# Two places for the weights of 256-column matmuls, and the last tile's transposes behind a unit of matmuls

## The chip, the cores and the metric

One NeuronCore of a Trainium2 chip runs the whole program. The metric is the device time of one execution in microseconds; the time given is the median of three runs. Matmuls run on TensorE, their results are in PSUM banks of 512 float32 per partition, and VectorE and ScalarE read them from there. SP issues the loads of the weights, GpSimd a few stores and memsets.

## The reference

A trunk of two layers on 512 tokens of 1024 channels, all float32. Layer 0 mixes tokens by stick-breaking attention (16 heads), layer 1 by a gated MLP over chunks of 128 tokens; behind each stands a SwiGLU feed-forward block of inner width 2816:

```
h = rms_norm(x, pre_g) * (1 + scale) + shift        # scale, shift, gate from c
y = mixer(h)            # attention in layer 0, gated token MLP in layer 1
x = x + gate * rms_norm(y, post_g)
h = rms_norm(x, ffn_pre_g) * (1 + scale') + shift'
y = (silu(h @ w_gate) * (h @ w_up)) @ w_down
x = x + gate' * rms_norm(y, ffn_post_g)
```

## The kernel before

**Precision.** A float32 operand is split into a high part in fp32r (ScalarE, a Copy) and a low part, the rest (VectorE, a subtraction). `mm3` makes three matmuls of each product: high by high, high by low, low by high. In the profile, wh and wl are the parts of a weight tile, hTh and hTl those of the transposed activations, Sh and Sl those of sums of them.

**Weights.** `stream` lists all weight tiles in the order of their use. `wload` issues the load of the next into `raw` (two buffers); `wemit` splits it into the buffers that `wtile` hands out in turn: five, and a sixth (`wpool2`) from the end of the attention on, each 1088 float32 long, one for the high and one for the low part. A tile has 1024 elements; `at` says how many elements into its buffer it begins. Tiles whose matmuls have 256 columns (`wgu`, `win_u` and the block tiles) begin at `SHORT` = 29, most others at 16, those of `down_blocks` at 0. `wget(key, look)` takes a tile and emits the splits of `look` more.

**Feed-forward.** The first three pairs of gate and up slabs are plain units (`Ffn.unit`): 48 matmuls of 256 columns into a bank `gu` for 256 tokens. The other 19 are done by `seven`, which makes seven half-size products where eight would be needed, 84 matmuls of 256 columns into banks r1 to r3, from block tiles `x`, `t13`, `t24` and `b21` that `blocks` works out of two raw loads (rawx, rawy). `b21` has its own buffers of 544 elements, two for each part.

**Boundary.** `out_proj` ends a sublayer. Its last four slabs of weights are used tile by tile of 128 tokens (tt = 0 to 3), and behind each tile stands `boundary`: ScalarE squares y (`junk<-y`), VectorE forms t = y * G, then x (`x<-t,r,x`), ScalarE squares x (`junk<-x`), VectorE forms t from x, A and B (this last operation is kept as `feature[0]`), TensorE transposes t in eight pieces (`tp<-identt,t`), and both halves are split into hTh and hTl. While the last two tiles go through it, TensorE has work on the first 256 tokens of the next sublayer, handed over as `nxt`: three plain units of gu, or two steps of v and one of u ahead of the gated MLP. `nxt[0]` stands ahead of the boundary of tile 2, `nxt[1]` ahead of that of tile 3, `nxt[2]` behind it.

**Order.** The order of each engine's work is set by a list scheduler when the program is built, by priority in program order and an estimate of when an operation is ready. `order(b, a)` holds b behind a without a wait. In the attention and in the `seven` stage the order on TensorE and VectorE is chained as written.

**Attention.** For each of eight head pairs, scores (`z`), scans on VectorE (`left<-ga,ones`), transposes (`tw`), splits (`ar`) and products with the values (`av`) alternate with steps of `filler`, three 512-column matmuls each: first the q and k of later pairs (`pqk`), then the first products of the output projection (`y`). `FILLS` gives the steps of each of seven slots for pairs 0 to 4, `LAST` for pairs 5 to 7. The sixth slot stands between the last flips and the scores of the next pair's last block; the first slot behind the pair's first transposes, the second behind the next pair's first scores.

Of the kernel before, what the change touches and what calls it, by code (L numbers as in the profile page):

```python
# [10 lines left out]
AF = mybir.ActivationFunctionType  # L11
# [15 lines left out]
SEVEN = ((2, 4, 6, 7, 9), (2, 4, 6, 7, 9, 10))  # L27
NLAST = 3

SHORT = 29  # L30


@with_exitstack
def trunk(ctx: ExitStack, tc: tile.TileContext, A: dict, out: bass.AP):
# [17 lines left out]
    def nm(s):  # L52
        uid[0] += 1
        return f"{s}_{uid[0]}"
# [7 lines left out]
    pe = {"prev": None, "chain": False}  # L62

    class Vector:


        chain, prev = False, None
# [13 lines left out]
    class Scalar:  # L81


        chain, prev = False, None
# [8 lines left out]
    act = Scalar()  # L93

    def pe_op(b):

        if pe["chain"] and pe["prev"] is not None:
            order(b, pe["prev"])
        pe["prev"] = b

    def order(b, before):
        tc.add_manual_dep(
            b.ins, before.ins.name,
            mybir.DependencyInfo(mybir.DependencyClass.NoSync, mybir.DependencyReason.DATA),
            reason="order",
        )
# [7 lines left out]
    last_tp = [None]  # L114

    def transpose(o, i):
        last_tp[0] = nc.tensor.transpose(o, i, ident)  # L117
        pe_op(last_tp[0])
# [18 lines left out]
    turn = [-1]  # L137
    wpools = [(wpool, 5)]
    fwork = {}
    last_low = [None]  # L140
# [3 lines left out]
    def wload():  # L144

        src, a, b, key = stream[len(raws)]
        if src is None:
            raws.append(block_loads(key[1]))
            return
        raw = wraw.tile([P, a, b], F32, tag="raw", name=nm("raw"))  # L150
        load(raw[:], src)
        raws.append(raw)

    def wemit():
        n = len(got)
        src, a, b, key = stream[n]
        if len(raws) == n:
            wload()
        if src is None:
            if not first_blocks or n > first_blocks[-1] + KF:  # L160
                first_blocks.append(n)
            for _ in blocks(*next_raws(n)):
                pass
            return
        raw = raws[n]
        if key[0] == "wdn" and key[2] in SEVEN[key[1]]:
            got.append(down_blocks(raw))
            return
        h, l = wtile(a, b, SHORT if key[0] in ("wgu", "win_u") else 16)
        if key[0] == "wqk" and key[1]:  # L170

            act.activation(h[:], raw[:], AF.Copy)
            nc.vector.tensor_tensor(l[:], raw[:], h[:].bitcast(F32), ALU.subtract)
            if len(raws) == n + 1 and stream[n + 1][3][0] == "wqk":
                wload()
        else:
            act.activation(h[:], raw[:], AF.Copy)
            last_low[0] = nc.vector.tensor_tensor(l[:], raw[:], h[:].bitcast(F32), ALU.subtract)  # L178
        got.append((h, l))

    def wtile(a, b, at=0):
        turn[0] = (turn[0] + 1) % sum(c for _, c in wpools)
        pool = wpools[0][0] if turn[0] < wpools[0][1] else wpools[1][0]
        return [
            pool.tile([P, 1088], F32R, tag=n, name=nm(n))[:, at : at + a * b].rearrange(
                "p (a b) -> p a b", a=a
            )
            for n in ("wh", "wl")
        ]
# [20 lines left out]
    def blocks(xr, yr):  # L210

        fp = fwork["pool"]

        def high(t, src):
            act.activation(t[0][:], src, AF.Copy)

        def low(t, src):
            dve.tensor_tensor(t[1][:], src, t[0][:].bitcast(F32), ALU.subtract)

        def half(t, i):  # L220
            return lambda k: (t[0][:, 4 * i + k, :], t[1][:, 4 * i + k, :])

        x = wtile(KD, P, SHORT)
        high(x, xr[:])
        f13 = fp.tile([P, KD, P], F32, tag="f13", name=nm("f13"))
        sum13 = dve.tensor_tensor(
            f13[:].rearrange("p (a k) f -> p a (k f)", a=2),
            xr[:].rearrange("p (a k) f -> p a (k f)", a=2),
            yr[:, 4:8, :].rearrange("p (a k) f -> p a (k f)", a=1).to_broadcast([P, 2, 512]),
            ALU.add,  # L230
        )
        if len(got) == first_blocks[-1]:
            order(sum13, feature[0])
        yield
        b21 = [
            fp.tile([P, 544], F32R, tag=f"b21{i}", name=nm("b21"))[
                :, SHORT : SHORT + 512
            ].rearrange("p (a b) -> p a b", a=4)
            for i in range(2)
        ]  # L240
        high(b21, yr[:, 0:4, :])
        t13 = wtile(KD, P, SHORT)
        high(t13, f13[:])
        f24 = fp.tile([P, KD, P], F32, tag="f24", bufs=1, name=nm("f24"))
        dve.tensor_tensor(f24[:, 0:4, :], f13[:, 0:4, :], xr[:, 4:8, :], ALU.add)
        dve.tensor_tensor(f24[:, 4:8, :], f24[:, 0:4, :], yr[:, 0:4, :], ALU.add)
        yield
        low(x, xr[:])
        low(b21, yr[:, 0:4, :])
        yield  # L250
        t24 = wtile(KD, P, SHORT)
        high(t24, f24[:])
        low(t13, f13[:])
        yield
        low(t24, f24[:])
        got.append({
            "B11": half(x, 0), "B22": half(x, 1), "B21": half(b21, 0),
            "T1": half(t13, 0), "T3": half(t13, 1), "T2": half(t24, 0), "T4": half(t24, 1),
        })

    feature = [None]
    first_blocks = []

    def ahead():
# [219 lines left out]
        lo %= 256  # L484
        return h[:, k % 4, lo : lo + n], l[:, k % 4, lo : lo + n]

    def boundary(s, tt, y, xin, hT, S, tag):

        halves = [slice(0, 512), slice(512, D)]
        sq = [small.tile([P, 1], F32, tag=f"sq{hf}", name=nm("sq")) for hf in range(2)]  # L490
        t = npool.tile([P, D], F32, tag="n", name=nm("t"))
        for hf, c in enumerate(halves):
            act.activation(junk[:, c], y[hf][:], AF.Square, accum_out=sq[hf][:])
            if hf == 1:
                sd, r2 = rms(sq[1][:], sq[0][:])
            dve.tensor_tensor(t[:, c], y[hf][:], ada["G", s][:, c], ALU.mult)
        dve.reciprocal(r2[:], sd[:])
        x = xin(tt)
        dve.scalar_tensor_tensor(x[:], t[:], r2[:, 0:1], x[:], ALU.mult, ALU.add)
        xd[tt] = dram.tile([P, D], F32, tag=f"x{tt}", bufs=2, name=nm("xd"))  # L500
        nc.gpsimd.dma_start(out=xd[tt][:], in_=x)
        sx = small.tile([P, 1], F32, tag="sx", name=nm("sx"))
        act.activation(junk[:], x[:], AF.Square, accum_out=sx[:])
        sd, r1 = rms(sx[:])
        dve.tensor_tensor(t[:], x[:], ada["A", s], ALU.mult)
        dve.reciprocal(r1[:], sd[:])
        feature[0] = dve.scalar_tensor_tensor(
            t[:], t[:], r1[:, 0:1], ada["B", s], ALU.mult, ALU.add
        )
        late = []  # L510
        for q in range(2):
            ps = bank("tp", tag)
            for k in range(4):
                kk = q * 4 + k
                transpose(ps[:, k * P : (k + 1) * P], t[:, kk * P : (kk + 1) * P])
            a = ps[:].rearrange("p (a b) -> p a b", a=4)
            if tt % 2 == 0:
                hT[tt // 2, q] = (slot(F32R, "hTh", 4, 256), slot(F32R, "hTl", 4, 256))
            c = slice(tt % 2 * P, (tt % 2 + 1) * P)
            th, tl = hT[tt // 2, q]  # L520
            split(th[:, :, c], tl[:, :, c], a)
            if S is not None and tt < 2:
                if tt == 0:
                    S["c", q] = slot(F32, "c", 4, 256)
                act.activation(S["c", q][:, :, tt * P : (tt + 1) * P], a, AF.Copy)
            late.append(a)
        return lambda: sums(S, tt, late)
# [33 lines left out]
    def out_proj(s, nk, get_act, wkey, J, bg, hT, nxt=(), pre=None, S=None, steps=0, bg2=None):  # L561
# [6 lines left out]
        mid = min(nk - J, -(-8 * len(bg.parts) // steps) + 1) if steps else None  # L568
        yp = None
        y = [[None, None] for _ in range(NT)]  # L570
# [39 lines left out]
        xin = xs.get  # L610
# [10 lines left out]
                xs[tt + 2] = x_load(tt + 2)  # L621
        evacs, late = [], []
        for n, tt in enumerate((2, 3)):
            if nxt:
                evacs.append(nxt[n]())
            late.append(boundary(s, tt, y[tt], xin, hT, S, "p" if tt == 3 else "b"))
        if nxt:
            evacs.append(nxt[2]())
            with tc.issue_after(last_sqrt[0].ins):
# [51 lines left out]
    hT = new_hT()  # L681
# [153 lines left out]
    with tc.tile_pool(name="att", bufs=1) as att, tc.tile_pool(name="att2", bufs=2) as att2:  # L835
# [44 lines left out]
        NEARLY = 4  # L880
        FIRST = (8, 9)
        FILLS = (2, 3, 2, 2, 2, 2, 3)
        LAST = (2, 2, 2, 2, 2, 1, 1), (1, 2, 1, 1, 1, 1, 1), (2, 0, 2, 0, 2, 2, 0)
        fgen = filler()

        def fill(n, at=None):
# [9 lines left out]
        for js in (B31, B2, B0):  # L896
            at, n = {}, 0
# [134 lines left out]
        for k in range(KD):  # L1032
# [9 lines left out]
            if k > 3:  # L1042
                tt = TURNS[k - 4]
# [17 lines left out]
        for i in range(NPAIR):  # L1061
            scores, flip, values, gather, part = cur
            more = i + 1 < NPAIR
            F = iter(FILLS if i < 5 else LAST[i - 5])
            flip(LATE, 0)
# [50 lines left out]
    junk = jpool.tile([P, D], mybir.dt.bfloat16, name="junk")  # L1116
# [532 lines left out]
```

## Time and profile before

| | |
|---|---|
| runs | 1106.79, 1112.53, 1112.93 us; median 1112.53 |
| profiled execution | 1114.39 us |
| its span | 1112.6 us |
| its granted TensorE clock | 0.997 |
| busy: TensorE, VectorE, ScalarE | 1090.5, 945.9, 593.1 us |
| DMA | 176.38 MB, mean 159 GB/s |

The profile is that of one execution. A group's row gives line, engine, operation, out<-in by the program's names, shapes and count, then the busy time and the mean duration of one in ns, then the idle time of the engine ahead of them and what ended it. A row of the timeline gives start and duration in us, and in brackets the idle time ahead of it with what ended it. A matmul overlaps the next one, so the rate is read from the distance of starts, or from a stretch divided by its count. L109 is the line in `mm` that issues every matmul, L117 the transposes, L87 ScalarE, L71 VectorE, L178 the low part of a streamed weight tile.

### The profile page before, as it was taken

How to read it: one execution, taken by the hardware profiler on the slowest of the kernel's cores; microseconds unless marked ns; L12 is line 12 of the kernel's file. 1: busy time of each engine (PE TensorE's matmuls, PEld its weight loads, DVE VectorE, ACT ScalarE, POOL GpSimd, SP SyncE). 2: the span in 40 equal slices, each digit the busy share in tenths (PEclk: the TensorE clock that was granted, in tenths of full speed). 3: DMA queues.
4: the chain of work that ended last, by engine and by line, in shares of the span. 5: the costliest groups of instructions: out<-in, count | busy, mean ns of one | idle time of the engine just before them, and what ended most of it. 6: DMA issues, size and time to landing. Idle time of an engine off the chain costs nothing.

```text
span 1112.6 us, 18514 instructions
## 1 busy us (share of the span) xinstructions
PE 1090.5 (98%) x7404; PEld 982.9 (88%) x7404; DVE 945.9 (85%) x1248; ACT 593.1 (53%) x982; POOL 29.5 (3%) x53
## 2 busy tenths in 40 slices
PE   6999999999999999999999999999999999999997
PEld 4787878788999999998888889988999999989995
DVE  4988999876989999989866967668979999899996
ACT  5445565665655555554243627426555555565652
POOL 0020100000000000000000000001000000000000
PEclk9999999999999999999999999999999999999999
DMA  8966433214423434459757465234334343332243
GB/s 303 363 224 212 137 124 117 92 57 151 153 98 126 163 127 151 133 186 356 272 190 259 138 228 183 82 116 160 120 110 160 125 162 104 107 112 95 79 140 123
DMA packets 51355, 176.38 MB, mean 159 GB/s; under 512 B 6074, under 2 KB 9146, under 8 KB 51268
## 3 DMA queue, kind: packets, MB, share of 16 engines
q1 hardware_dynamic: 48708, 166.81, 43.9%
q0 software_dynamic: 2560, 8.39, 2.0%
q8 instruction: 58, 0.95, 0.3%
q14 instruction: 29, 0.24, 0.1%
HBM read 164.69 MB, written 8.39 MB: 156 GB/s over the span
## 4 chain that ended last, share of the span: by engine, by line
PE 82%; DVE 9%; ACT 4%; DMA 3%; issue 2%; SPq 0%; DVEq 0%; ACTq 0%
PE r L109 31%; PE y L109 17%; PE v L109 8%; PE pqk L109 7%; PE u L109 4%; PE gu L109 4%; PE av L109 2%; PE z L109 2%; PE tw L117 1%; DMA raw<-in_wdn 1%; DVE wl L71 1%; DVE al L71 1%; PE tp L117 1%; DVE wl L178 1%; PE ab L109 1%
## 5 line engine op out<-in xcount | busy, mean ns | idle before, releaser
L87 ACT ACTIVATE wh<-raw 128x1024 fp32r<-128x1024 f32 (+1 forms) x112 | 115.7, 1037 | 136.8 <-PE y L109 38.7
L109 PE MATMUL r<-Sh,wh 128*128 128x256 f32 x608 | 168.1, 276 | 0.0
L109 PE MATMUL r<-Sh,wl 128*128 128x256 f32 x608 | 167.9, 276 | 0.0
L109 PE MATMUL r<-Sl,wh 128*128 128x256 f32 x608 | 167.9, 276 | 0.0
L109 PE MATMUL y<-wh,as 128*128 128x512 f32 x480 | 150.0, 390 | 0.0
L178 DVE TENSOR_TENSOR wl<-raw,wh 128x1024 fp32r<-128x1024 f32 x87 | 105.9, 1222 | 48.5 <-ACT wh L87 47.8
L109 PEld LDWEIGHTS r<-Sh,wh 128*128 128x128 f32 x608 | 114.1, 188 | 0.3 <-ACT e L87 0.2
L109 PEld LDWEIGHTS r<-Sl,wh 128*128 128x128 f32 x608 | 114.2, 188 | 0.1
L109 PEld LDWEIGHTS r<-Sh,wl 128*128 128x128 f32 x608 | 114.1, 188 | 0.0
L109 PEld LDWEIGHTS y<-wh,as 128*128 128x128 f32 x480 | 90.0, 188 | 18.7
L71 DVE TENSOR_TENSOR wl<-f,wh 128x1024 fp32r<-128x1024 f32 x87 | 103.3, 1221 | 1.4 <-ACT wh L87 1.4
L87 ACT ACTIVATE wh<-f 128x1024 fp32r<-128x1024 f32 x87 | 91.8, 1056 | 20.0 <-DVE f L71 11.8
L87 ACT ACTIVATE e<-r 128x256 f32<-128x256 f32 x114 | 43.8, 385 | 102.6 <-PE r L109 100.4
L109 PE MATMUL y<-wl,as 128*128 128x512 f32 x240 | 93.7, 390 | 0.0
L109 PE MATMUL r<-hTh,wh 128*128 128x256 f32 x304 | 84.2, 277 | 0.2 <-DVE gu L71 0.2
L109 PE MATMUL r<-hTh,wl 128*128 128x256 f32 x304 | 84.0, 276 | 0.0
L109 PE MATMUL r<-hTl,wh 128*128 128x256 f32 x304 | 84.0, 276 | 0.0
L109 PE MATMUL r<-hTh,b 128*128 128x256 f32 x304 | 58.0, 276 | 0.0
L109 PEld LDWEIGHTS r<-hTh,wh 128*128 128x128 f32 x304 | 57.1, 188 | 0.9 <-DVE gu L71 0.9
L87 ACT ACTIVATE wh<-rawx 128x1024 fp32r<-128x1024 f32 x38 | 40.5, 1065 | 32.0 <-PE r L109 29.0
L109 PEld LDWEIGHTS r<-hTl,wh 128*128 128x128 f32 x304 | 57.1, 188 | 0.0
L109 PEld LDWEIGHTS r<-hTh,wl 128*128 128x128 f32 x304 | 57.1, 188 | 0.0
(260 smaller groups left out, 2943.6 us busy)
## 6 DMA issues: line engine op xcount, KB each, us to landing
rawada<-in_ada SPq DMA_DIRECT2D x80, 512.0 KB, 5.8
rawy<-in_wy SPq DMA_DIRECT2D x38, 512.0 KB, 4.4
rawx<-in_wx SPq DMA_DIRECT2D x38, 512.0 KB, 4.2
raw<-in_wdown SPq DMA_DIRECT2D x22, 512.0 KB, 5.5
raw<-in_wdn SPq DMA_DIRECT2D x22, 512.0 KB, 3.7
raw<-in_wqk SPq DMA_DIRECT2D x16, 512.0 KB, 4.1
ada<-in_ada0p SPq DMA_DIRECT2D x12, 512.0 KB, 7.6
raw<-in_wgu SPq DMA_DIRECT2D x12, 512.0 KB, 3.5
```

Of the source, the lines that this page charges most:

```text
L71: b = getattr(nc.vector, op)(*args, **kw)
L87: b = nc.scalar.activation(*args, **kw)
L109: b = nc.tensor.matmul(o, l, r, start=start, stop=stop, skip_group_check=True)
L117: last_tp[0] = nc.tensor.transpose(o, i, ident)
L178: last_low[0] = nc.vector.tensor_tensor(l[:], raw[:], h[:].bitcast(F32), ALU.subtract)
```

## The change

`SHORT` becomes the pair 29, 61; `wtile` takes one or the other by the turn of the buffer, while `b21` stays at 29. For tile 3 the unit `nxt[1]` moves into `boundary`, between the last operation on t and the transposes (`mid`); the first transpose is held behind the unit's last matmul. The splits of the weight tiles that are emitted in there are held behind the boundary's own work, if they are tiles of `wgu`: the high part behind the Square of x, the low part behind t. In `LAST` one step of the filler goes from the second slot of pair 6 to the sixth of pair 5.

```diff
-SHORT = 29
+SHORT = 29, 61
...
-            act.activation(h[:], raw[:], AF.Copy)
+            high = act.activation(h[:], raw[:], AF.Copy)
             last_low[0] = nc.vector.tensor_tensor(l[:], raw[:], h[:].bitcast(F32), ALU.subtract)
+            if edge[0] and key[0] == "wgu":
+                order(high, feature[1])
+                order(last_low[0], feature[0])
...
     def wtile(a, b, at=0):
         turn[0] = (turn[0] + 1) % sum(c for _, c in wpools)
         pool = wpools[0][0] if turn[0] < wpools[0][1] else wpools[1][0]
+        if at is SHORT:
+            at = SHORT[turn[0] % 2]
...
-                :, SHORT : SHORT + 512
+                :, SHORT[0] : SHORT[0] + 512
...
-    def boundary(s, tt, y, xin, hT, S, tag):
+    def boundary(s, tt, y, xin, hT, S, tag, mid=None):
...
-        act.activation(junk[:], x[:], AF.Square, accum_out=sx[:])
+        feature[1] = act.activation(junk[:], x[:], AF.Square, accum_out=sx[:])
...
+        if mid is not None:
+            mid()
+            chain = pe["prev"]
         for q in range(2):
             ps = bank("tp", tag)
             for k in range(4):
                 kk = q * 4 + k
                 transpose(ps[:, k * P : (k + 1) * P], t[:, kk * P : (kk + 1) * P])
+                if mid is not None and kk == 0:
+                    order(last_tp[0], chain)
...
         for n, tt in enumerate((2, 3)):
-            if nxt:
-                evacs.append(nxt[n]())
-            late.append(boundary(s, tt, y[tt], xin, hT, S, "p" if tt == 3 else "b"))
+            def mid():
+                edge[0] = True
+                evacs.append(nxt[1]())
+                edge[0] = False
+
+            if nxt and tt == 2:
+                evacs.append(nxt[0]())
+            late.append(
+                boundary(
+                    s, tt, y[tt], xin, hT, S, "p" if tt == 3 else "b",
+                    mid if nxt and tt == 3 else None,
+                )
+            )
...
-        LAST = (2, 2, 2, 2, 2, 1, 1), (1, 2, 1, 1, 1, 1, 1), (2, 0, 2, 0, 2, 2, 0)
+        LAST = (2, 2, 2, 2, 2, 2, 1), (1, 1, 1, 1, 1, 1, 1), (2, 0, 2, 0, 2, 2, 0)
```

More of the change, by code (lines that the diff above doesn't have):

```diff
@@ L259, in blocks @@
         })
-    feature = [None]
+    feature = [None, None]
+    edge = [False]
     first_blocks = []
```

## The prediction

> **What bounds the kernel now.** I read the page first, then the chain in order of time, then the instruction groups and timelines of the stretches that the change touches.
>
> ```profile
> span 1112.6 us, 18514 instructions
> PE 1090.5 (98%) x7404; PEld 982.9 (88%) x7404; DVE 945.9 (85%) x1248; ACT 593.1 (53%) x982; POOL 29.5 (3%) x53
> PE 82%; DVE 9%; ACT 4%; DMA 3%; issue 2%; SPq 0%; DVEq 0%; ACTq 0%
> ```
>
> TensorE sets the time: 82% of the chain is its own work. A change can save only what a matmul takes or the few places where TensorE stands. The diff aims at both. First the matmuls, from the chain (start, duration, what, count):
>
> ```profile
> 294.77 22.32 PE gu L109 x186
> 317.09 167.92 PE r L109 x1476
> 675.99 23.04 PE u L109 x192
> 785.38 21.81 PE gu L109 x192
> 807.19 167.28 PE r L109 x1476
> ```
>
> All of these are 256-column matmuls of one form, yet they have two rates. 22.32 us / 186 and 23.04 / 192 are 120.0 ns each; 21.81 / 192 is 113.6 and 167.28 / 1476 is 113.3. The clock is not the reason; in this view of two stretches the third number from the right is the granted clock (the count takes in what overlaps the edges):
>
> ```profile
> 676.00:698.00 22.00, 22.00 (x185) 1.00 0.48 147
> 787.00:807.00 20.00, 20.00 (x179) 1.00 0.33 107
> ```
>
> Neither is it the code: gu runs at 120 ns in the first layer and at 113 in the second. A stretch enters one rate or the other and stays there. The 120 ns rate of the first layer ends soon after 327 us, and the instruction groups of three stretches show where (mean ns of one is the number behind the comma; 283 to 284 goes with 120 ns, 276 with 113; the first row is from 318 to 327 us, the second from 327 to 329, the last two from 330 to 480):
>
> ```profile
> L109 PE MATMUL r<-hTh,b 128*128 128x256 f32 x8 | 1.6, 284 | 0.0
> L109 PE MATMUL r<-hTh,b 128*128 128x256 f32 x8 | 1.6, 280 | 0.0
> L109 PE MATMUL r<-hTh,b 128*128 128x256 f32 x124 | 23.7, 276 | 0.0
> L109 PE MATMUL r<-Sh,wh 128*128 128x256 f32 x256 | 70.7, 276 | 0.0
> ```
>
> The first b product (tile b21 of the first block) leaves the rate at 284; the second b product breaks it, and after it all are at 276. What differs is the place. Weight buffers are 1088 elements long (4352 bytes, 17 times 256), so every one lies the same way against a 256-byte grid. The b buffers are 544 long (2176 bytes, eight and a half times 256), so with two buffers a tag the second block's b lies 128 bytes off. I read this as: a switch of the weights' place by 128 bytes throws TensorE out of the 120 ns rate, and, by the last two rows, leaves the 113 ns rate alone.
>
> **The change part by part.**
>
> *Offsets.* 61 less 29 is 32 elements, the same 128 bytes. With neighbouring tiles 29 and 61 in, every step from a gate tile to an up tile, or from one u tile to the next, is such a switch; nothing is added, only addresses move. What the 120 ns rate costs now: gu in the first layer 186 x 6.7 ns = 1.24 us, the r stage behind it 167.92 - 167.28 = 0.64 us more than its twin, u 192 x 6.7 = 1.28. The first plain unit of each layer (48 matmuls) runs at it too:
>
> ```profile
> L109 PE MATMUL gu<-hTh,wl 128*128 128x256 f32 x16 | 4.5, 284 | 0.0
> ```
>
> (280.5 to 286 us), 0.32 us in each. Half a u unit at 651 us belongs to a single tile and stays. If the rate lasts to the first change of tile only, 24 matmuls (0.16 us) stay of the gu stretch, 48 (0.32) of u and 24 of each first unit; about ten matmuls of settling cost 0.05 us each time. Saved: 1.24 + 0.64 - 0.16 - 0.05 = 1.67; 1.28 - 0.32 - 0.05 = 0.91; twice 0.11. Sum 2.8; I take 2.6, since a stretch can also come out of a wait in either rate. Bounds: 0, if the rate locks again at the new place, and 4.0, if it never starts (1.24 + 0.64 + 1.28 + 0.64, with the half unit's 0.16).
>
> Here the Trainium skill speaks against the edit: "TensorE: Matmul & The Clock Gate", Part 2, step 1, says that the array reads moving data and weights through two ports of their own, so that loading the next weights takes nothing from the running matmul; by that the place could not matter, and this term would be 0. The two rates above do not show such independence, but none of the rows proves that the place is the cause.
>
> *The boundary.* In the two boundaries ahead of gu, TensorE waits for the last tile's t:
>
> ```profile
> 292.88 0.28 PE L109 MATMUL gu<-hTh,wl 128*128 128x256 f32 x1
> 293.68 1.09 PE L117 MATMUL tp<-identt,t 128*128 128x128 f32 x8 [0.52 <-DVE t L71]
> 782.84 0.28 PE L109 MATMUL gu<-hTh,wl 128*128 128x256 f32 x1
> 784.29 1.09 PE L117 MATMUL tp<-identt,t 128*128 128x128 f32 x8 [1.17 <-DVE t L71]
> ```
>
> t is late because weight splits stand among its steps:
>
> ```profile
> 287.52 1.06 ACT L87 ACTIVATE wh<-raw 128x1024 fp32r<-128x1024 f32 x1 [0.31 <-DMA raw<-in_wgu]
> 288.49 1.04 ACT L87 ACTIVATE junk<-x 128x1024 bf16<-128x1024 f32 x1
> ...
> 285.53 1.28 DVE L71 SCALAR_TENSOR_TENSOR x<-t,r,x 128x1024 f32<-128x1024 f32 x1
> 286.73 1.22 DVE L178 TENSOR_TENSOR wl<-raw,wh 128x1024 fp32r<-128x1024 f32 x1
> 287.87 0.68 DVE L71 TENSOR_TENSOR hTl<-tp,hTh 128x512 fp32r<-128x512 f32 x1
> 288.61 1.23 DVE L178 TENSOR_TENSOR wl<-raw,wh 128x1024 fp32r<-128x1024 f32 x1
> 290.13 0.69 DVE L71 TENSOR_TENSOR hTl<-tp,hTh 128x512 fp32r<-128x512 f32 x1 [0.29 <-ACT hTh L87]
> 290.74 1.22 DVE L71 TENSOR_TENSOR t<-x,A 128x1024 f32<-128x1024 f32 x1
> 292.35 1.28 DVE L71 SCALAR_TENSOR_TENSOR t<-t,r,B 128x1024 f32<-128x1024 f32 x1
> ```
>
> The fifth and sixth weight tiles are emitted inside the second unit, so with the edit the wh at 287.52 goes behind the Square of x and the wl at 288.61 behind t; the wl at 286.73 is the fourth tile's and stays. Then the Square runs at 287.2, where ScalarE is free. VectorE goes on from 287.95 with t<-x,A, two hTl, a reciprocal and t: 1.22 + 0.68 + 0.69 + 0.15 + 1.28 = 4.0 us, so t stands at about 292.0 and not 293.6. The second unit's 48 matmuls end at 292.3 (54 run in the old piece, which ends at 293.0). The transposes follow without a wait; the old order had six matmuls of the third unit there as cover, and they now come behind. Gain: the idle 0.52 and a restart, 0.65. Queued behind the moved splits: the fifth tile's wl now ends at 292.0 + 1.22 = 293.2, where the third unit starts (its third matmul is the first that reads wl, 0.3 us later); the sixth's wl by 294.4, needed at 296. On SP, the sixth raw load waits for the fourth wl, which stays; the first block's rawx waits for the fifth wl, 3.3 us later than now, and is used only from 317. Were one more operation of 1.2 us put ahead of the fifth wl, the third unit would wait 0.9 and 0.25 be lost on balance.
>
> In the second layer:
>
> ```profile
> 776.58 1.22 DVE L178 TENSOR_TENSOR wl<-raw,wh 128x1024 fp32r<-128x1024 f32 x1
> 778.73 1.23 DVE L178 TENSOR_TENSOR wl<-raw,wh 128x1024 fp32r<-128x1024 f32 x1 [0.93 <-ACT wh L87]
> 782.95 1.28 DVE L71 SCALAR_TENSOR_TENSOR t<-t,r,B 128x1024 f32<-128x1024 f32 x1
> ```
>
> The same 4.0 us from 777.8 put t at 781.8, ahead of the unit's end at 783.0: the whole 1.17 goes. The boundary between the layers takes the new transpose order but no order on its splits; there the wait was about 0.1:
>
> ```profile
> 637.04 0.28 PE L109 MATMUL u<-hTh,wl 128*128 128x256 f32 x1
> 637.27 1.06 PE L117 MATMUL tp<-identt,t 128*128 128x128 f32 x8
> ```
>
> I take 0.1 there, 0 to 0.2. The term: 0.65 + 1.17 + 0.1 = 1.9, between -0.3 (that loss, and nothing gained elsewhere) and 2.0.
>
> *The filler.* The edit of LAST moves one step (three 512-column matmuls) from the second slot of head pair 6 to the sixth of pair 5. Pair 7's k is then finished ahead of the scores of pair 6's last block. Now its low half stands behind a scan on VectorE, and the z of pair 7 waits for it:
>
> ```profile
> 217.97 2.30 DVE L71 TENSOR_TENSOR_SCAN left<-ga,ones 128x1025 f32<-128x1025 f32 x1 [1.13 <-ACT ga L87]
> 220.18 0.67 DVE L71 TENSOR_TENSOR k<-pqk,k 128x512 fp32r<-128x512 f32 x1
> ...
> 220.90 1.01 PE L109 MATMUL z<-k,q 64*128 64x128 f32 x10 [0.65 <-DVE k L71]
> ...
> 222.19 1.02 DVE L71 SCALAR_TENSOR_TENSOR ar<-tw,ar 128x384 fp32r<-128x384 f32 x2
> ```
>
> With the edit k's low half fits into the 1.13 us in which VectorE waits for ga, and the 0.65 of TensorE goes. But the three matmuls before that z put ga and so the scan about 0.7 later: it ends at 220.95, two gathers of 0.7 follow, and the first ar low comes at 222.9, where it now is ready at 222.75. The av behind it, without a wait, would now be wanted at about 222.45. So about 0.45 comes back as a wait for ar. I take -0.2; bounds -0.65 (no new wait) and +0.5 (the scans behind it slip too, by the old stall's size less what was saved).
>
> *Sum.* 2.6 + 1.9 + 0.2 = 4.7 us. The profiled execution took 1114.39 us, its span 1112.6 with 1.8 around it that nothing here touches: 1109.7. The median of the runs, 1112.53, lies 1.9 below that execution, so a median of about 1107.8 follows.
>
> **The rivals.**
>
> *The place is nothing.* The 120 ns rate is a matter of when a stretch starts, and the second b product broke it by chance; or it locks again at the new place. Then only boundary and filler count: 1112.5 - 2.1 = 1110.4. For it: five stretches enter the 120 ns rate and others of the same form and the same buffers do not, which timing explains as well. Against: the first b product, in the same place as the rest, leaves the rate alone, and the second, 128 bytes off, does not. This is also what the two ports of the Trainium skill's page, cited above, would give.
>
> *The 113 ns rate is lost.* One mechanism on the other side: in the r stage x, t13 and t24 now alternate between both places, 12 matmuls at a time, and each switch throws TensorE out of the rate that it has. Two layers of 19 blocks of 84 matmuls are 3192; all at 120 ns cost 3192 x 6.7 ns = 21 us: 1112.5 - 2.1 + 21 = 1131. It decides from some 700 matmuls on, where it has eaten the 4.7 us, and is over 1% from about 2000. For it: at 327 a switch did disturb the rate. Against: the b row from 330 to 480, half of whose blocks lie 128 bytes off, stands at 276 like the others.
>
> *The boundary gives nothing.* The order holds the splits back so long that the third unit waits where the transposes waited, and the filler's new wait is as long as the old: 1112.5 - 2.6 + 0.3 + 0.5 = 1110.7. For it: the fifth wl ends within 0.3 us of its need in the first layer. Against: the second layer has about 1.1 us of room.
>
> *More than the sum.* All terms at their upper bounds, 4.0 + 2.0 + 0.65 = 6.7, with the executions falling like the quickest of the three shown (1106.79): 1100.1. For it: one of three was there. Against: the other two lie 6 us higher, and no row shows where.
>
> **How the numbers follow.** The forecast has 0.52, the place 0.18, the boundary 0.12, the lost rate 0.07, more than the sum 0.11. The predicted time is the forecast's, 1107.8. With all terms at their bounds the forecast reaches from 1105.8 (6.7 saved) to 1113.3 (no gain from the offsets, 0.3 and 0.5 lost); the runs shown lie 6 us apart. I give 1100 to 1114, which leaves out the lost rate and little else. A measurement of this kernel can tell about 1%, 11 us, from no change: faster than 1101.4 holds only in the last case, 0.11; slower than 1123.7 only in the lost rate, 0.07; the rest, 0.82, is within.
>
> **What would show it.** Offsets: the chain rows of gu in the first layer and of u with 192 matmuls near 113.8 to 116 ns each, not 120, and r at 167.3 in both layers. Boundary: the transposes of the last tile without an idle for t, eight of them right behind 48 matmuls of gu, and the third unit's first matmuls without a wait for wl. Filler: no 0.65 at z, and less than that at the next av. The prediction is wrong if gu or u still run whole at 120, if rows of r rise above 276, or if the idle for t comes back as one for wl.

## The result and the profile after

The changed kernel takes 1108.14 us (median of 22 runs, 1105.92 to 1111.52), the kernel before 1109.80 in 22 runs beside it (1106.79 to 1113.34). The ratio is 0.9983, 95% interval 0.9975 to 0.9991: faster by 1.9 us, 1.0 to 2.8. The prediction's 1107.8 was near, but its sum was 4.7 us: the median of the three runs that it started from lay 2.7 us above that of the longer series, and that hid most of the difference.

The profiled execution of the changed kernel has a span of 1104.1 us, that of before 1112.6. Some 4 us of these 8.5 come from work that the change does not touch, the loads and first products ahead of the attention, which take from 84.5 to 89.1 us in profiles of kernels that are alike there. So I compare stages.

The chain in order of time, after (start, duration, what, count), for the 256-column stretches that the prediction showed:

```profile
289.08 21.89 PE gu L109 x192
315.60 163.48 PE r L109 x1440
669.92 22.33 PE u L109 x192
776.95 21.92 PE gu L109 x192
798.88 167.28 PE r L109 x1476
```

gu of the first layer runs at 114.0 ns a matmul where this one profile of before has 120, u at 116.3 instead of 120, r of the second layer as before, and gu there at 114.2 where it was 113.6. The r row of the first layer begins behind a wait; 36 matmuls of r stand ahead of it. More of this wait below.

The last transposes of both boundaries, after, on TensorE:

```profile
287.73 0.28 PE L109 MATMUL gu<-hTh,wl 128*128 128x256 f32 x1
287.99 1.09 PE L117 MATMUL tp<-identt,t 128*128 128x128 f32 x8
288.84 0.37 PE L109 MATMUL gu<-hTh,wh 128*128 128x256 f32 x1
...
775.80 0.28 PE L109 MATMUL gu<-hTh,wl 128*128 128x256 f32 x1
775.92 1.03 PE L117 MATMUL tp<-identt,t 128*128 128x128 f32 x8
```

No idle in brackets any more: the 0.52 and the 1.17 are gone. On VectorE the splits now stand behind t:

```profile
281.11 1.28 DVE L71 SCALAR_TENSOR_TENSOR x<-t,r,x 128x1024 f32<-128x1024 f32 x1
282.31 1.22 DVE L178 TENSOR_TENSOR wl<-raw,wh 128x1024 fp32r<-128x1024 f32 x1
283.44 1.51 DVE L71 TENSOR_TENSOR hTl<-tp,hTh 128x512 fp32r<-128x512 f32 x2
284.87 1.22 DVE L71 TENSOR_TENSOR t<-x,A 128x1024 f32<-128x1024 f32 x1
...
286.66 1.28 DVE L71 SCALAR_TENSOR_TENSOR t<-t,r,B 128x1024 f32<-128x1024 f32 x1
287.86 2.35 DVE L178 TENSOR_TENSOR wl<-raw,wh 128x1024 fp32r<-128x1024 f32 x2
```

From the start of x to the end of t it is 6.8 us, where it was 8.1; t ends at 287.94, when the unit's last matmul has just started. Two waits of TensorE are new in the list of waits (engine and line, what it waited for, us in total, times, longest), and one of VectorE for the raw loads of the block tiles; those of z for k and of the transposes for t are gone:

```profile
PE av L109 <- DVE ar L71: 0.8, 1, 0.8
PE r L109 <- ACT e L87: 0.5, 1, 0.5
DVE f L71 <- DMA rawx<-in_wx: 1.2, 2, 0.7
```

### The profile page after: what moved, and what is told of

Its sections match the earlier page's. It is cut to its first block, busy times and chain, and to the rows that moved or that the text cites. A ratio compares the mean times of both kernels' runs of the same rounds, so it can differ in the third digit from the quotient of the medians.

```text
span 1104.1 us, 18512 instructions
## 1 busy us (share of the span) xinstructions
PE 1083.9 (98%) x7404; PEld 978.6 (89%) x7404; DVE 945.3 (86%) x1248; ACT 592.7 (54%) x982; POOL 29.5 (3%) x53
## 4 chain that ended last, share of the span: by engine, by line
PE 84%; DVE 8%; ACT 3%; DMA 3%; issue 2%; SPq 0%; DVEq 0%; ACTq 0%
PE r L109 31%; PE y L109 17%; PE v L109 8%; PE pqk L109 7%; PE gu L109 6%; PE u L109 4%; PE av L109 2%; PE z L109 2%; PE tw L117 1%; DVE wl L71 1%; DMA raw<-in_wdn 1%; DVE al L71 1%; PE tp L117 1%; DVE f L71 1%; DVE Sl L71 1%
```

## The experiments

All have the kernel before as their base unless the text says otherwise. The table gives stages of each profile in us, each the distance between the starts of two TensorE instructions in the timeline: first gu to first r in the two layers; first r to the first y behind it (layer 0); first v of the gated MLP to its last v; from there to the last u; first pqk to last av (attention). "again" and "after2" are second profiles of the kernel before and of the changed one.

| | before | again | off | bound | nohold | last | after | after2 | swap |
|---|---|---|---|---|---|---|---|---|---|
| gu to r, layer 0 | 36.72 | 35.61 | 35.40 | 35.91 | 35.20 | 35.67 | 35.06 | 35.05 | 35.20 |
| r to y, layer 0 | 181.09 | 180.50 | 180.56 | 180.82 | 180.80 | 180.88 | 181.28 | 181.66 | 181.61 |
| v to last v | 50.93 | 50.93 | 50.77 | 50.88 | 50.88 | 50.93 | 50.63 | 50.63 | 50.88 |
| last v to last u | 44.53 | 44.51 | 43.79 | 44.57 | 44.51 | 44.53 | 43.77 | 43.79 | 43.71 |
| gu to r, layer 1 | 36.21 | 36.07 | 36.13 | 34.80 | 35.56 | 36.15 | 34.73 | 34.49 | 34.75 |
| attention | 156.9 | 156.8 | 156.5 | 156.5 | 156.4 | 156.5 | 156.5 | 156.5 | 157.5 |

**off: the offsets alone.**

```diff
-SHORT = 29
+SHORT = 29, 61
...
         pool = wpools[0][0] if turn[0] < wpools[0][1] else wpools[1][0]
+        if at is SHORT:
+            at = SHORT[turn[0] % 2]
...
-                :, SHORT : SHORT + 512
+                :, SHORT[0] : SHORT[0] + 512
```

> The kernel before with the two offsets alone (29 and 61 in turn, b21 at 29). Place theory: a change of the weights' place by 128 bytes throws TensorE out of the 120 ns rate. Then gu of the first layer (192 matmuls) and u (192) take no more than 114 to 117 ns each, whichever rate they start in, r stays at 113.3, the waits for t of 0.5 and 1.2 us stay, and the time falls by 1 to 2.6 us. Rival, the rate is a matter of timing alone: some stretch of gu or u still runs at 120 over more than two tiles, and the time stays within 0.5 us.

Ratio 0.9989 (0.9974 to 1.0004): 1.2 us less, but the interval takes in no change at all, so the stages decide. The instruction groups show how u loses its 120 ns rate; the rows are those of its first tile, its second and the last two (672.7 to 678.1, 678.2 to 683.6, 684.2 to 695 us):

```profile
L109 PE MATMUL u<-hTh,wh 128*128 128x256 f32 x16 | 4.5, 283 | 0.0
L109 PE MATMUL u<-hTh,wh 128*128 128x256 f32 x16 | 4.5, 281 | 0.0
L109 PE MATMUL u<-hTh,wh 128*128 128x256 f32 x32 | 8.8, 276 | 0.0
```

The first tile, at 29, runs at 120 as before. The switch to 61 does not end it: that tile runs whole at 118.2 ns (281). The switch back ends it. So a switch changes the rate at once, as the place theory says, but the second place has a rate of its own above 113. The saving in the stage up to the last u is 44.52 - 43.79 = 0.73 us, and 0.7 to 0.8 in every profile with the offsets in turn. One gain ahead of that stage is the offsets' too: the half unit of u among the v products, at 651 us in the profile of before, which the prediction left as it was, now lies at 61 and takes 2.74 us, where it took 2.88.

**bound: the boundary alone.** The changed kernel with `SHORT = 29, 29` and the old `LAST`.

> The kernel before with the boundary edit alone (unit inside the boundary, splits held back, transposes behind the unit; all tiles at 29, LAST as before). By the prediction's sum the idle of 0.5 and 1.2 us ahead of the last transposes goes and the time falls by 1.9 us (1.4 to 2.0). Rival: the third unit waits for its weights instead and the time stays within 0.5. A stretch of gu at 120 ns from unit to unit may still occur, since nothing breaks it but a wait or transposes.

Ratio 0.9985 (0.9972 to 0.9997), 1.7 us less (0.3 to 3.1). In the second layer the stage falls by 1.3 to 1.4 us (36.07 to 36.21 before, 34.80 here), and no wait for t is left in either layer. In the first layer this profile has some 225 matmuls at 117.7 ns, from the transposes to a pause in the r stage, which hides the boundary's part there; all their tiles lie at 29, and none of the changes of tile broke the rate.

**nohold: the boundary without the two order calls.**

```diff
-            if edge[0] and key[0] == "wgu":
+            if edge[0] and key[0] == "none":
```

(against bound)

> The boundary edit alone, all weights at 29, without the two order calls that hold the splits of the gate and up tiles behind the boundary's Square and t. Theory of the prediction: the splits in the chain of t are what made t late, so t is late again, the idle ahead of the last transposes comes back (up to 0.5 and 1.2 us) and the time is at most 1 us under before. Rival: the place of the unit in program order is enough, since it already puts the splits behind: first gu to r 34.8 in the second layer as with them.

Ratio 1.0000 (0.9987 to 1.0014). The wait for t is back in part:

```profile
PE tp L117 <- DVE t L71: 0.8, 2, 0.5
```

The stage of the second layer is 35.56, half of the way. So there the moved unit alone takes half of the idle, and holding the splits takes the rest: the theory of the splits in the chain of t holds, and the rival (program order is enough) does not. This rests on the waits and the stage; the intervals of the times of bound and nohold overlap. In the first layer the unit alone already brings the stage to 35.20.

**last: the moved filler step alone.**

```diff
-        LAST = (2, 2, 2, 2, 2, 1, 1), (1, 2, 1, 1, 1, 1, 1), (2, 0, 2, 0, 2, 2, 0)
+        LAST = (2, 2, 2, 2, 2, 2, 1), (1, 1, 1, 1, 1, 1, 1), (2, 0, 2, 0, 2, 2, 0)
```

> The kernel before with the moved filler step alone. Prediction: the 0.65 us at z goes, about 0.45 comes back at the next av as a wait for ar, time -0.2 us (-0.65 to +0.5). Rival: the wait only changes place, 0.0. Over 0.7 us either way would mean that something behind it shifts too.

Ratio 1.0000 (0.9986 to 1.0013); the attention takes 156.5 us, in kernels without the edit 156.4 to 157.3 (the longest is wide, below). The wait only changes place. In the changed kernel's timelines, k's low half fits ahead of the scan as foreseen, the scan starts later, and av waits for ar:

```profile
214.08 0.68 DVE L71 TENSOR_TENSOR k<-pqk,k 128x512 fp32r<-128x512 f32 x1
214.68 2.28 DVE L71 TENSOR_TENSOR_SCAN left<-ga,ones 128x1025 f32<-128x1025 f32 x1
216.88 1.38 DVE L71 TENSOR_TENSOR of<-av,of 64x512 f32<-64x512 f32 x2
218.30 1.02 DVE L71 SCALAR_TENSOR_TENSOR ar<-tw,ar 128x384 fp32r<-128x384 f32 x2
```

and on TensorE:

```profile
218.91 1.08 PE L109 MATMUL av<-ar,U 128*128 128x128 f32 x7 [0.78 <-DVE ar L71]
```

This run gave something else. Its profile has a pause in the first block of the r stage, behind which r runs at 120 ns. The groups from 317 to 321.4, of the second block's b (321.6 to 322.9) and from 324.5 to 340 us:

```profile
L109 PE MATMUL r<-Sh,wh 128*128 128x256 f32 x9 | 2.5, 283 | 0.0
L109 PE MATMUL r<-hTh,b 128*128 128x256 f32 x8 | 1.6, 280 | 0.0
L109 PE MATMUL r<-Sh,wh 128*128 128x256 f32 x32 | 8.8, 276 | 0.0
```

The second block's b breaks the rate again, as in the profile of before.

**bsame: all b tiles in the weights' place.**

```diff
-            fp.tile([P, 544], F32R, tag=f"b21{i}", name=nm("b21"))[
-                :, SHORT : SHORT + 512
-            ].rearrange("p (a b) -> p a b", a=4)
+        b21 = fp.tile([P, 1088], F32R, tag="b21", name=nm("b21"))
+        b21 = [
+            b21[:, SHORT + 512 * i : SHORT + 512 * i + 512].rearrange("p (a b) -> p a b", a=4)
```

> The kernel before, with both parts of b21 in one buffer of 1088 elements (29 to 541 and 541 to 1053), so that the b tiles of all blocks lie in the same place against the 256-byte grid as the other weights; no other edit. Place theory: where gu of a layer enters the r stage at 120 ns, nothing in the stage breaks it any more; if it lasts, the stage of 1596 matmuls takes 10.7 us more. So r of the first layer is near 178 us where it was 167.9, or unchanged at 113.3 ns where gu came in at 113. Timing theory: the second block breaks the rate as before, the stage stays at 168 us and the time within 1 us.

Ratio 1.0002 (0.9984 to 1.0021), r at 113.3 in both layers. gu came in at 113 here, so the run does not tell the theories apart.

**wide, widesame, wideoff: an entry made to order.** Four matmuls of 512 columns ahead of the r stage; the second also with b21 as in bsame, the third with the offsets of off.

```diff
             rest = None
+            pe["chain"] = True
+            wide, hs = bank("wide", "p"), self.hT[0, 0][0]
+            for j in range(4):
+                mm(wide[:], hs[:, 0, 0:P], hs[:, 0:2, :], j == 0, j == 3)
```

> The kernel before, all weights at 29, with four extra matmuls of 512 columns (into an unused bank) between the last plain unit and the first block of the r stage in each layer; everywhere else in the profiles a 256-column stretch straight behind 512-column ones begins at 120 ns. So r should begin at 120 in both layers. Place theory: it ends in the second block's b product (some 96 matmuls, then a dozen to settle), cost 0.9 us for the extra matmuls and 0.7 for the rate in each layer, 3 us in all. Timing theory: it ends anywhere or not at all, the same in the next kernel.

> As the last, with both parts of b21 in one buffer of 1088 elements, so that all weights of the r stage lie in one place against the 256-byte grid. Place theory: nothing breaks the 120 ns rate, and both r stages of 1596 matmuls run at 120: near 178 us each where they took 167.5, 2 x 10 us above the kernel before it, ratio about 1.02. Timing theory: as the last kernel, within 1 us of it.

> The four extra 512-column matmuls with the weights at 29 and 61 in turn (b21 at 29). Place theory: the tiles of the first block already lie in two places, so the 120 ns rate is over within the first block (84 matmuls), 0.2 to 0.5 us for each layer beside the 0.9 of the extra matmuls, a little under the first of the three. Timing theory: no difference from it.

Ratios 1.0011 (0.9997 to 1.0025), 1.0023 (1.0001 to 1.0045) and 1.0004 (0.9987 to 1.0021). All three missed: r did not begin at 120. Behind the extra matmuls its first distances were 115, 123, 113, 120, 118, 117 and 114 ns, then 113, in five of the six entries (the second layer of wideoff wandered between 114 and 121 for some thirty). Five hundred and twelve columns ahead are not enough to bring the rate about; the forecast of 10 us a layer was therefore never put to the test.

**all61: one place, the other one.** `61` instead of `SHORT` in all calls of `wtile`, b21 at 29.

> The kernel before with every tile of 256-column matmuls at 61 and b21 at 29, nothing in turn. It asks whether 61 is a better place or the switch is what helps. Switch: u (192 matmuls behind 512-column ones) runs whole at one rate above 117 ns, as it does whole at 120 with 29; time as before within 1 us, or lower by at most 0.4 if that rate is 118. Better place: u runs at 113.3 from the start, 1.3 us less there and 0.3 in each first unit.

Ratio 0.9995 (0.9981 to 1.0008). The chain has u at

```profile
672.00 21.77 PE u L109 x192
```

which is 113.4 ns from its start: the rate at entry depends on the place of the first tile, which neither answer had foreseen in full. But 118.2 ns now turns up elsewhere, in 126 later matmuls of u and in 138 of r. In this kernel the b tiles of the second block lie in the place of the others and those of the third 128 bytes off. Groups of the second block's b (322.8 to 324), of 326 to 331, of the third block's b (332.8 to 334) and of 336 to 340 us:

```profile
L109 PE MATMUL r<-hTh,b 128*128 128x256 f32 x8 | 1.6, 281 | 0.0
L109 PE MATMUL r<-Sh,wh 128*128 128x256 f32 x15 | 4.2, 281 | 0.0
L109 PE MATMUL r<-hTh,b 128*128 128x256 f32 x8 | 1.5, 278 | 0.0
L109 PE MATMUL r<-Sh,wh 128*128 128x256 f32 x12 | 3.3, 276 | 0.0
```

Here the second block's b leaves the rate alone and the third block's breaks it: the block moved with the places. Chance would have to hit the right block in three profiles out of three. This, with off, decides for the place theory, in stretches that came about by accident. It does not make the switch necessary for the saving: all61 has 43.78 us from the last v to the last u, as the kernels with the offsets in turn have, without a switch among the tiles of u.

**again: the kernel before once more.** No edit.

> The kernel before, unchanged, for a second profile. If the 120 ns stretch of gu in the first layer (186 matmuls and the first block and a half of r) is an accident of one execution, it is not here: from the first gu to the first r some 35.5 us where the first profile has 36.7, and r at 167.3. Rival, it is the usual course of that kernel: 36.7 and 167.9 again. In both cases u (192) takes 23.04 us and the span from the first gu of the second layer to its r 36.1.

One execution, 1110.61 us; its r stages take

```profile
292.43 21.11 PE gu L109 x186
313.54 167.33 PE r L109 x1476
671.96 23.04 PE u L109 x192
```

gu runs at 113.5 and r at 113.4. The 120 ns stretch of gu in the first profile was an accident of that execution; u at 120 is the rule. The same holds in last, bsame, wide and widesame, whose weights also lie at 29: u takes 23.04 us in each, and gu of the first layer is at 113 in each behind its transposes.

**after2: the changed kernel once more.** No edit.

> The changed kernel, unchanged, for a second profile. What repeats is the change's own: u 22.3 us, first gu to r 35.0 and 34.7 us in the two layers, no idle for t. The idle of 0.6 in the r stage of the first layer (for e) repeats if the moved splits cause it (theory: the early block preparation is late), and is gone if it is an accident. Time -1.9 us against before, as in the 22 runs.

Ratio 0.9984 (0.9973 to 0.9996). The stages repeat within 0.4 us, and so does the wait for e. It is not an accident. Around it, the timeline of ScalarE and VectorE, and then the list of waits of that stretch (311 to 316.6 us):

```profile
315.53 0.66 ACT L87 ACTIVATE e<-r 128x256 f32<-128x256 f32 x2 [1.08 <-DVE act L71]
...
313.87 1.22 DVE L71 TENSOR_TENSOR wl<-f,wh 128x1024 fp32r<-128x1024 f32 x1
315.00 0.74 DVE L71 TENSOR_TENSOR act<-silu,gu 128x256 f32<-128x256 f32 x2
```

```profile
ACT e L87 <- DVE act L71: 1.1, 1, 1.1
PE r L109 <- ACT e L87: 0.6, 1, 0.6
```

In the first block of the r stage VectorE works without a pause (from 310.6 to 315.7 in that timeline), and e waits behind it. TensorE comes to this block 0.5 us earlier than in again, and what the boundary saved in the first layer is given back there. bound and off have no such wait; the three profiles with the offsets, the boundary and the filler together have it (0.5, 0.6 and 0.8).

VectorE is late there as well, because it was idle once earlier. `f<-rawx,rawy` adds two raw loads, an early step in preparing a block of the r stage; this is the second such sum of the first layer, in before and in after:

```profile
298.54 1.22 DVE L71 TENSOR_TENSOR f<-rawx,rawy 128x1024 f32<-128x1024 f32 x1
294.53 1.22 DVE L71 TENSOR_TENSOR f<-rawx,rawy 128x1024 f32<-128x1024 f32 x1 [0.66 <-DMA rawx<-in_wx]
```

The load of the first block's rawx goes out behind the splits that are held back, 13.4 us after the first gu where it was 9.8 in again. This idle stands in every profile in which the splits are held (after 0.66, after2 0.18 and 0.53, bound 0.85, swap 1.15 us) and not in before, again, off or nohold. Counted from the first gu, e starts at 39.2 us in again, 39.0 in off and nohold, but at 39.4, 39.5 and 39.8 in after, after2 and swap. An early TensorE alone does not make the wait: all61 comes to the block as early as the changed kernel (34.93 us), finds e at 38.8 and is idle for 0.02. In bound e is late too (39.7), but there the 117.7 ns stretch brings TensorE late enough to find it ready. By these figures the wait comes from both, an earlier TensorE and block loads that the held splits delay; the changed kernel without the hold, which would separate them, was not run.

**swap: the changed kernel with the offsets exchanged.**

```diff
-SHORT = 29, 61
+SHORT = 61, 29
...
-                :, SHORT[0] : SHORT[0] + 512
+                :, SHORT[1] : SHORT[1] + 512
```

> The changed kernel with the two offsets exchanged (61 for even turns, 29 for odd, b21 at 29). With 61 for all tiles u ran at 113.4 from its start, so the place of the first tile behind the 512-column matmuls sets the rate of entry. Expected: u 21.8 us and not 22.3, the first unit of the first layer at 113 to 115, that of the second layer at 120 for its gate half; 0.4 us less than the changed kernel, which only the stages of the profile can show. Rival, the entry is by timing: u enters at 120 as before.

Ratio 0.9983 (0.9971 to 0.9995). u enters at 61 and takes 21.78 us, as forecast, and the first unit of the first layer 5.46; that of the second layer starts at 120 (5.71). But the stage up to the last u gains 0.1 only, since later tiles of u fall into 118.2, and gu of the first layer has 78 matmuls at 118.1. No version tried beats the changed kernel by more than the measurement can tell.

## Why the prediction was right or wrong

*The direction and the size* were right: faster, within 1%. That the changed kernel's time was met within 0.4 us is luck, two errors against each other: the start, taken from three runs, 2.7 us too high, and the sum, 2.8 too large.

*Offsets: 2.6 forecast, about 0.9 found (0.73 at u, 0.16 in the v stage ahead of it).* The mechanism was right in the main: the place matters, a switch of 128 bytes changes the rate of TensorE at once, and r keeps its 113 ns with tiles in two places (167.28 us in the second layer, to the digit). But a switch does not always lead to 113: in off it led from 120 to 118.2 first, and in swap gu of the first layer passed two switches at about 118 and left that rate only at the third. The step that failed is the sum of what 120 ns cost "now": 1.24 + 0.64 us of gu and r in the first layer were taken from one execution as the rule, though the text said that stretches enter either rate. With what was to stay they made 1.67 of the 2.8 us. The second profile of the same kernel has these stretches at 113.5 and 113.4. Of the terms that do recur, u gave 0.73 and not 0.91, because the second tile does not settle at 113 but runs whole at 118.2.

*The boundary: 1.9 forecast, and about as much taken from the waits.* In the second layer bound gave 1.3 to 1.4 (1.17 forecast). In the middle it gave 0.05 (0.1 forecast): of the 0.3 in the changed kernel 0.16 shows with off alone, and about 0.1 is open. In the first layer the stage is 0.55 shorter than in again and 0.34 shorter than in off, which has the offsets too (0.65 forecast). nohold shows that the chain of t was the cause. The step that failed is the one on what is late behind the moved splits. The prediction saw that the first block's rawx would go out 3.3 us later (it was 3.6) and put that at nothing, because rawx "is used only from 317". That is when its matmuls start; VectorE reads it from 294.7 in the profile of before, and from 300 on, to the end of the first block, it has no pause over 0.3 us in which a delay could be made up. There 0.5 to 0.6 came back as the wait for e. In the first layer holding the splits gained nothing that the table shows: from the first gu to the first y it is 216.1 us in again, 216.0 in nohold, 216.3 and 216.7 in the changed kernel.

*The filler: -0.2 forecast, 0.0 found.* The new wait at av was foreseen at 0.45; it is 0.8, and the old one was 0.65. So the step that failed is the size of the new wait; the bounds took in the result.

*The rivals.* "The place is nothing" is out by the three b products and by u in off. "The 113 ns rate is lost" did not happen in r. "The boundary gives nothing" holds for the first layer alone: the held splits cost about what they gained, though at the block loads and not at the third unit, and the filler's wait only changed its place, as this rival said. "More than the sum" did not happen. Put together from the stages of after and again: -0.55 + 0.78 - 0.30 - 0.74 - 1.34 - 0.3 = -2.4 us (after2: -2.2), inside the measured 1.0 to 2.8. The last term is the attention, where last found no effect, so it is chance. Of what "r to y" lost (0.78 in after, 1.16 in after2) the new wait is 0.5 and 0.6; the rest I did not trace, apart from 66 matmuls at 118 in after2 (0.3 us). The 118 ns rates that the change itself brings were in no term of the sum.

## What to carry to other kernels

A rate that one profile shows in one stretch is a term of the sum only if it has a cause that recurs; a second profile of the same kernel would have taken 1.7 us out of this sum. Where work is moved behind a critical chain, follow what waits for it, loads included, to the first instruction that reads the result on any engine, and not only on the one that sets the time. And look at the next engine that is busy without a pause: what it loses earlier, and what is saved ahead of it, comes back there as a wait. Where equal matmuls run at different rates, compare the addresses of the tiles at the point where the rate changes.

## What the runs showed of the hardware

Identical 256-column matmuls ran at four steady rates, 113.3, 117.7, 118.2 and 120.0 ns, at a granted clock of 0.997 to 0.999, and kept one for 130 matmuls and more. The rate changed at a pause, at transposes, or at a switch of the stationary tiles by 128 bytes; with all tiles at 29 a stretch behind the v products was at 120 in all eight profiles, and with its first tile at 61 at 113.4 in the two that have it there (all61, swap). The same switch never slowed a stretch that ran at 113.3. Why the place acts so is open: neither the addresses of the moving tiles nor other distances than 128 bytes were tried.
